# A Hyena and attention encoder layer: the short sequence's second DFT stage computed in quarters of the array, and the filter's real and imaginary parts each stored twice

## The chip, the cores and the metric

The kernel runs on one core of a Trainium2 chip. The metric is device time in microseconds (us) of one execution, lower is better; several runs are taken and the median is compared. The core's engines are named as in the profile: PE (TensorE, matmuls; PEld is its weight load), DVE (VectorE), ACT (ScalarE), POOL (GpSimd) and SP (SyncE, which here only issues DMAs).

## The reference

One encoder layer is applied with the same weights to two sequences: the prompt, 1024 positions (sequence A in the kernel), and the sample, 512 positions (sequence B), both with 1024 channels. After a modulated RMS norm one projection feeds a Hyena branch (768 channels), a dilated attention branch and two gates. The gated branch outputs are merged, projected and added to the input; a squared-ReLU MLP follows. Everything is float32. The change lies in the Hyena branch, a convolution as long as the sequence, whose filter is itself computed by a small network from position features:

```python
def implicit_filter(L, w1, b1, ..., w_out):
    ...
    h_fwd, h_bwd = jnp.split(h, 2, axis=-1)
    h_fwd, h_bwd = h_fwd * decay, h_bwd * decay
    k2 = jnp.concatenate([h_fwd, jnp.zeros((1, D_HYENA), f32), h_bwd[1:][::-1]], axis=0)
    return k2 / jnp.sum(jnp.abs(k2), axis=0, keepdims=True)

def long_conv(u, k2, d):
    L = u.shape[1]
    uf = u.astype(jnp.float32)
    U = jnp.fft.rfft(uf, n=2 * L, axis=1)
    K = jnp.fft.rfft(k2, n=2 * L, axis=0)
    y = jnp.fft.irfft(U * K[None], n=2 * L, axis=1)[:, :L]
    return (y + uf * d.astype(jnp.float32)).astype(u.dtype)

def hyena_branch(z, conv_w, conv_b, ...):
    ...
    x0, x1, v = jnp.split(zc, 3, axis=-1)
    k2 = implicit_filter(L, ...)
    return x0 * long_conv(x1 * v, k2, hyena_d)
```

## The kernel before

**The main stream.** The big projections are a list of units, run in order by `stream` (L483). A unit loads a 128-column piece of a weight (`wdma`, L468), splits it on ACT and DVE into a high and a low fp32r part (`split`, called at L480; ACT's cast is L401, DVE's subtraction L402), and multiplies it in `mm3` (L762), three products for each tile; the matmuls are at L768. Unit i+1's weight is split when unit i begins. The units come in this order: qkv and z of A (`qkvA`, `zhyA`), gates of A (`gateA`), `qkvB`, `zhyB`, `gateB`, then `mixA`, `mixB` (merge and output projection), `ffA`, `ffB`.

**The side work.** Filters (`filtA`, `filtB`), convolutions (`convA`, `convB`), attention, norms and the loading of the Hyena output for the merge (`load_y`, the DMA at L1425) are generators. `pump` advances them between the steps of the units; each `yield` states a cost and a latency on a planned clock, and that clock decides where in the program a piece of side work is written. `LLD` (8.0) is the time that a stage-two step allows for its loads, `LY` (6.0) the time between the product with the filter and the backward DFT. The context holds ACT to the order in which the program is written (`manual_schedule` with the Activation engine). The instructions of the other engines are placed by the framework's scheduler.

**The long convolution.** A transform of 2L points is done in two stages of 32 and Q = L/16 points: Q is 64 for A and 32 for B. Each third of the 768 channels (256 channels) is a step of its own. Stage one goes out to a DRAM tile, stage two reads it back in another order. In stage two a group `eg` holds four 128-row tiles of 256 channels, and each tile is multiplied by its own 128 x 128 matrix (`cmat`, L907, a pool of four buffers). For A (Q = 64) the 128 rows are the real and imaginary part of one residue. For B (Q = 32) they are the real and imaginary parts of two residues l = 0, 1, in the order (part, l, q), and the matrix has zeros wherever the two residues would mix, in half of its entries. A float32 product of 128 x 128 by 256 columns shows as two MATMUL records.

- The filter, `filt_third` (L827): stage one is at L867 in 64 x 64 quarters of the array; stage two (L890 to L902) multiplies at L899, scales on DVE at L900 and stores the spectrum with one DMA of 128 rows per group at L902 into `S.spec[th]`, real rows first, imaginary rows behind.
- The convolution, `conv_gen` (L927): `middle` (L966) loads four pieces of the spectrum (L971, L972), so that `ka` holds the real part in both halves and `kb` the imaginary part in both halves; loads two matrices; multiplies forward at L984, by the spectrum on DVE at L985 to L988, and backward at L995; ACT copies the result (L996, recorded at the helper's line L388) and the stores are at L1001. Each group is handled as two halves `ep` of two tiles with a `yield` between them. Groups of one convolution follow one another (`WMID` is 1). Behind the last group the result is read back at L1008 and multiplied at L1020.
- A has four groups per third, B two. So B has six filter steps, six forward and six backward products, each of four tiles.

These products write to PSUM tiles that `pss2` takes from a pool of four buffers.

## Time and profile before

| what | value |
|---|---|
| median of 3 runs | 2627.82 us (2626.16 to 2630.31) |
| the profiled execution, its own time | 2630.32 us |
| its span, first to last instruction | 2628.5 us |
| mean granted TensorE clock | 0.990 |
| ACT busy | 860.8 us (33%) |
| DMA moved | 351.06 MB, queue q1 busy for 41.1% of 16 engines' span |
| PE work of filter B | from 866.8 to 1086.5 us |
| PE work of convolution B | from 1102.4 to 1362.6 us |

The profile is one execution. A group row gives the line, the engine, the operation, the tiles written and read (`filtB__s` is a PSUM tile that the filter of B made), the shape, the count, then busy time and mean duration, and behind the second bar how long the engine was idle before these instructions and what ended that idle time. A row of the timeline gives the start in us from the span's start, the duration in us, the engine, the line and the count of merged instructions, in brackets the idle time before. A row of the windows gives, for each stretch, its length, the busy time of PE, PEld, DVE, ACT and POOL with counts, the granted clock, the share of the DMA engines and GB/s.

### The profile page before, as it was taken

How to read it: one execution, taken by the hardware profiler on the slowest of the kernel's cores; microseconds unless marked ns; L12 is line 12 of the kernel's file. 1: busy time of each engine (PE TensorE's matmuls, PEld its weight loads, DVE VectorE, ACT ScalarE, POOL GpSimd, SP SyncE). 2: the span in 40 equal slices, each digit the busy share in tenths (PEclk: the TensorE clock that was granted, in tenths of full speed). 3: DMA queues.
4: the chain of work that ended last, by engine and by line, in shares of the span. 5: the costliest groups of instructions: out<-in, count | busy, mean ns of one | idle time of the engine just before them, and what ended most of it. 6: DMA issues, size and time to landing. Idle time of an engine off the chain costs nothing.

```text
span 2628.5 us, 31915 instructions
## 1 busy us (share of the span) xinstructions
PE 2562.4 (97%) x12872; PEld 2061.4 (78%) x12872; DVE 1248.1 (47%) x1626; ACT 860.8 (33%) x1398; POOL 152.0 (6%) x122
## 2 busy tenths in 40 slices
PE   8999999999899999999899989999999999999999
PEld 4677788787788677787788868888888888888887
DVE  4354443744657644653455563333333332554544
ACT  5544323532422444443332442112211221323232
POOL 0111000000010310000022210000000000000000
PEclk9999999999999999999899999999999999999999
DMA  7455575556565344557563531111111112322223
GB/s 269 143 158 182 185 192 169 151 177 175 190 229 188 110 161 141 157 177 233 190 214 114 189 100 61 48 48 49 48 48 48 49 48 80 129 97 96 98 95 104
DMA packets 138106, 351.06 MB, mean 134 GB/s; under 512 B 19016, under 2 KB 50303, under 8 KB 137830
## 3 DMA queue, kind: packets, MB, share of 16 engines
q1 hardware_dynamic: 137670, 348.22, 41.1%
q8 instruction: 102, 1.67, 0.3%
q0 software_dynamic: 288, 0.79, 0.1%
q14 instruction: 46, 0.38, 0.0%
HBM read 280.67 MB, written 71.16 MB: 134 GB/s over the span
## 4 chain that ended last, share of the span: by engine, by line
PE 50%; DVE 1%; DMA 1%; ACT 0%; issue 0%; SPq 0%; DVEq 0%; ACTq 0%
PE ffA__mm L768 27%; PE ffB__mm L768 13%; PE mixA__mm L768 6%; PE mixB__mm L768 2%; PE convB__s L1020 0%; DMA mixA__g<-zhyA__dr 0%; PE gateB__mm L768 0%; DVE mixB__wl L402 0%; ACT mixB__wh L401 0%; PE convB__s L995 0%; DVE mixA__g L402 0%; PE convB__s L984 0%; DMA convB__g<-convB__dr 0%; DVE normA__g L735 0%; DVE mixB__g L1491 0%
## 5 line engine op out<-in xcount | busy, mean ns | idle before, releaser
L768 PE MATMUL ffA__mm<-ffA__g,ffA__wh 128*128 128x512 f32 x1024 | 274.1, 389 | 0.0
L768 PE MATMUL ffA__mm<-normA__g,ffA__wh 128*128 128x512 f32 x992 | 265.1, 389 | 0.0
L768 PEld LDWEIGHTS ffA__mm<-ffA__g,ffA__wh 128*128 128x128 f32 x1024 | 192.0, 188 | 40.4 <-issue 0.4
L768 PEld LDWEIGHTS ffA__mm<-normA__g,ffA__wh 128*128 128x128 f32 x992 | 186.2, 188 | 38.6
L1529 DVE SCALAR_TENSOR_TENSOR mixA__g<-ffA__mm,adam,mixA__g 128x1024 f32<-128x1024 f32 x64 | 82.1, 1283 | 190.1 <-PE ffA__mm L768 190.1
L768 PE MATMUL ffB__mm<-ffB__g,ffB__wh 128*128 128x512 f32 x512 | 157.8, 389 | 0.0
L768 PE MATMUL ffA__mm<-ffA__g,ffA__wl 128*128 128x512 f32 x512 | 157.7, 389 | 0.0
L768 PE MATMUL ffB__mm<-normB__g,ffB__wh 128*128 128x512 f32 x496 | 152.7, 389 | 0.0
L768 PE MATMUL ffA__mm<-normA__g,ffA__wl 128*128 128x512 f32 x496 | 152.7, 389 | 0.0
L401 ACT CAST ffA__wh<-ffA__wr 128x1024 fp32r<-128x1024 f32 x63 | 66.2, 1051 | 256.7 <-PE ffA__mm L768 213.6
L768 PE MATMUL zhyA__mm<-init__g,zhyA__wh 128*128 128x512 f32 x512 | 145.2, 400 | 0.0
L1511 DVE SCALAR_TENSOR_TENSOR ffA__g<-ffA__mm,ffA__g 128x1024 f32<-128x1024 f32 x32 | 39.2, 1224 | 222.8 <-ACT ffA__g L1510 222.8
L768 PE MATMUL gateA__mm<-init__g,gateA__wh 128*128 128x512 f32 x480 | 133.4, 398 | 7.5 <-ACT gateA__wh L401 7.5
L768 PE MATMUL mixA__mm<-mixA__g,mixA__wh 128*128 128x512 f32 x424 | 115.3, 392 | 3.1 <-DVE mixA__g L1463 1.9
L768 PE MATMUL qkvA__mm<-init__g,qkvA__wh 128*128 128x512 f32 x416 | 116.9, 399 | 0.0
L768 PEld LDWEIGHTS zhyA__mm<-init__g,zhyA__wh 128*128 128x128 f32 x512 | 94.2, 188 | 23.6 <-issue 5.7
L768 PEld LDWEIGHTS ffB__mm<-ffB__g,ffB__wh 128*128 128x128 f32 x512 | 96.0, 188 | 20.3 <-ACT ffB__g L401 0.2
L768 PEld LDWEIGHTS gateA__mm<-init__g,gateA__wh 128*128 128x128 f32 x480 | 90.5, 191 | 27.2 <-ACT gateA__wh L401 7.9
L768 PEld LDWEIGHTS ffA__mm<-ffA__g,ffA__wl 128*128 128x128 f32 x512 | 96.1, 188 | 20.0
L1510 ACT ACTIVATE ffA__g<-ffA__mm 128x1024 f32<-128x1024 f32 x32 | 32.9, 1029 | 237.8 <-PE ffA__mm L768 237.8
L768 PEld LDWEIGHTS ffB__mm<-normB__g,ffB__wh 128*128 128x128 f32 x496 | 93.1, 188 | 19.4
L768 PEld LDWEIGHTS ffA__mm<-normA__g,ffA__wl 128*128 128x128 f32 x496 | 93.1, 188 | 19.3
(499 smaller groups left out, 4926.7 us busy)
## 6 DMA issues: line engine op xcount, KB each, us to landing
ada__g<-ada SPq DMA_DIRECT2D x32, 512.0 KB
ffA__wr<-w_up SPq DMA_DIRECT2D x32, 512.0 KB
ffA__wr<-w_dn SPq DMA_DIRECT2D x32, 512.0 KB
ffB__wr<-w_dn SPq DMA_DIRECT2D x32, 512.0 KB
ffB__wr<-w_up SPq DMA_DIRECT2D x30, 512.0 KB
filtA__dr<-filtA__g SPq DMA_DIRECT2D x24, 512.0 KB
convA__g<-filtA__dr SPq DMA_DIRECT2D x48, 256.0 KB
init__g<-ada SPq DMA_DIRECT2D x16, 512.0 KB
```

The source lines that it names most:

```text
L401: A.copy(hi, raw)
L768: T.matmul(ps[:, 512 * c:512 * c + 512], ww[:, sl], xx(k)[:, 512 * c:512 * c + 512], start=k == 0 and p == 0, stop=k == kt - 1 and p == 2)
L1510: A.activation(r, ps[:, :L], AF.Relu)
L1511: V.scalar_tensor_tensor(r, ps[:, :L], 0.0, r, ALU.max, ALU.mult)
L1529: V.scalar_tensor_tensor(S.h(m), ps[:, :L], mod(S, 5, m), S.h(m), ALU.mult, ALU.add)
```

## The change

For B the rows of stage two are put in the order (l, part, q), so that each 128 x 128 matrix is two 64 x 64 blocks. Only these blocks are kept; a group's matrices shrink from 256 KB to 128 KB. A new function, `stage2_products`, replaces the three places that multiplied in stage two. For A it issues what stood there. For B it takes two PSUM buffers at once and issues the eight 64 x 64 products of a group in one go, in the quarter pattern of L867; in tiles 2 and 3 of a group the two residues come out in swapped halves, and the backward matrices are stored with swapped blocks to bring them back.

For both sequences the filter stores its spectrum as two DRAM tiles, the real part twice and the imaginary part twice, so that the convolution loads `ka` and `kb` with one DMA each. In the filter, A's store is two DMAs of 512 KB per group, B's four of 256 KB.

In B's convolution the two DVE operations on 64 partitions (L986, L987) become four on 32 partitions.

```diff
@@ _stage2
     for m in (fw, bw):
-        m = m.reshape(ntile // 4, 4, 128, 128).transpose(0, 2, 1, 3)
+        if nl == 2:
+            m = np.stack([m[:, :, l, :, :, l, :].reshape(ntile, 64, 64) for l in range(2)], axis=1)
+            if out:
+                m[2::4], m[3::4] = m[2::4, ::-1].copy(), m[3::4, ::-1].copy()
+        m = m.reshape(ntile // 4, 4, 128, 128 // nl).transpose(0, 2, 1, 3)
@@ filt_gen
-        S.spec = [dram((128, nt, 256)) for _ in range(3)]
+        S.spec = [[dram((128, nt, 256)) for _ in range(2)] for _ in range(3)]
@@ filt_third, stage2
             so = g((4, 256))
-            for ep in range(2):
-                ps = pss2()
-                for ee in range(2):
-                    e = 2 * ep + ee
-                    T.matmul(ps[:, ee], cm[:, e], sin[:, e], start=True, stop=True)
+            for ep, ps in stage2_products(S, cm, sin):
                 V.tensor_tensor(so[:, 2 * ep:2 * ep + 2], ps, rn.unsqueeze(1).broadcast_to([128, 2, 256]), ALU.mult)
                 yield 0.9, 0.0
-            dma(S.spec[th][:, 4 * eg:4 * eg + 4], so)
+            for l in range(64 // Q):
+                b0 = stage2_row(S, 0, l)
+                for r, dt in enumerate(S.spec[th]):
+                    p0 = stage2_row(S, r, l)
+                    dma(dt[b0:b0 + 2 * Q, 4 * eg:4 * eg + 4].rearrange("(d q) e c -> q d e c", d=2),
+                        so[p0:p0 + Q].unsqueeze(1).broadcast_to([Q, 2, 4, 256]))
@@ cmat
         cm = wp.tile([128, 4, 128], F32, tag="cm", name=nm("cm"), bufs=4)
+        if src.shape[-1] == 64:
+            cm = cm[:, 0:2].rearrange("p a (b c) -> p (a b) c", b=2)
         dma(cm, src[eg])
         return cm
+    def stage2_row(S, r, l):
+        return 64 * r + S.Q * l if S.Q == 64 else 64 * l + S.Q * r
+
+    def stage2_products(S, w, x):
+        if S.Q == 64:
+            for ep in range(2):
+                ps = pss2()
+                for ee in range(2):
+                    T.matmul(ps[:, ee], w[:, 2 * ep + ee], x[:, 2 * ep + ee], start=True, stop=True)
+                yield ep, ps
+            return
+        ps = pss2(), pss2()
+        for ee in range(2):
+            for ep in range(2):
+                for h in range(2):
+                    o, rs = 64 * (h ^ ep), slice(64 * h, 64 * h + 64)
+                    T.matmul(ps[ep][o:o + 64, ee], w[rs, 2 * ep + ee], x[rs, 2 * ep + ee], start=True, stop=True)
+        yield from enumerate(ps)
@@ stage2_load, and the stores of middle
-                p0 = 64 * r + Q * l
+                p0 = stage2_row(S, r, l)
@@ conv_gen, middle
-            for hf in range(2):
-                dma(ka[64 * hf:64 * hf + 64], S.spec[th][0:64, es])
-                dma(kb[64 * hf:64 * hf + 64], S.spec[th][64:128, es])
+            for t, dt in zip((ka, kb), S.spec[th]):
+                dma(t, dt[:, es])
             if eg == 0:
-                V.tensor_copy(ka[64:65, 0], kb[0:1, 0])
+                V.tensor_copy(ka[Q:Q + 1, 0], kb[0:1, 0])
                 V.memset(kb[0:1, 0], 0.0)
-                V.memset(kb[64:65, 0], 0.0)
+                V.memset(kb[Q:Q + 1, 0], 0.0)
             cm, cb_ = cmat(S.fw, eg), cmat(S.bw, eg)
             yield 0.0, LLD
             y, vv = g((4, 256)), g((4, 256))
-            for ep in range(2):
+            for ep, ps in stage2_products(S, cm, sin):
                 e2 = slice(2 * ep, 2 * ep + 2)
-                ps = pss2()
-                for ee in range(2):
-                    T.matmul(ps[:, ee], cm[:, 2 * ep + ee], sin[:, 2 * ep + ee], start=True, stop=True)
                 V.tensor_tensor(y[:, e2], ps, ka[:, e2], ALU.mult)
-                V.scalar_tensor_tensor(vv[0:64, e2], ps[64:128], -1.0, kb[0:64, e2], ALU.mult, ALU.mult)
-                V.tensor_tensor(vv[64:128, e2], ps[0:64], kb[64:128, e2], ALU.mult)
+                for l in range(nl):
+                    re, im = (slice(stage2_row(S, r, l), stage2_row(S, r, l) + Q) for r in range(2))
+                    V.scalar_tensor_tensor(vv[re, e2], ps[im], -1.0, kb[re, e2], ALU.mult, ALU.mult)
+                    V.tensor_tensor(vv[im, e2], ps[re], kb[im, e2], ALU.mult)
                 V.tensor_tensor(y[:, e2], y[:, e2], vv[:, e2], ALU.add)
                 yield 0.9, LY if ep else 0.0
             del sin, ka, kb, vv
             so = g((4, 256))
-            for ep in range(2):
-                ps = pss2()
-                for ee in range(2):
-                    T.matmul(ps[:, ee], cb_[:, 2 * ep + ee], y[:, 2 * ep + ee], start=True, stop=True)
+            for ep, ps in stage2_products(S, cb_, y):
                 copy(so[:, 2 * ep:2 * ep + 2], ps)
                 yield 0.9, 0.0
```

More of the change, by code (lines that the diff above doesn't have):

```diff
@@ L827, in filt_third @@
     def filt_third(S, th, sall, fwo):
-        J, nt = S.J, S.nt
+        J, Q, nt = S.J, S.Q, S.nt
         cs = slice(256 * th, 256 * th + 256)
@@ L999, in middle @@
                 for l in range(nl):
-                    p0 = 64 * r + Q * l
+                    p0 = stage2_row(S, r, l)
                     dma(v2[r, l][:, 4 * eg:4 * eg + 4], so[p0:p0 + Q])
```

## The prediction

> **What bounds the kernel now.** I read the page's busy times first, then the windows by stage, then single groups and the timeline at the places that the change touches.
>
> ```profile
> span 2628.5 us, 31915 instructions
> PE 2562.4 (97%) x12872; PEld 2061.4 (78%) x12872; DVE 1248.1 (47%) x1626; ACT 860.8 (33%) x1398; POOL 152.0 (6%) x122
> ```
>
> PE is the bound over the whole; DVE and ACT have room on the average. An average isn't enough, so here are the stretches: filter A, filter B, convolution B up to 1235 us, and a short one behind it. The columns are length, PE, PEld, DVE, ACT and POOL busy, clock, DMA share and GB/s.
>
> ```profile
> 120.00:310.00 190.00, 185.48 (x1315) 142.85 (x1315) 92.02 (x129) 73.75 (x164) 25.48 (x26) 1.00 0.56 178
> 900.00:1090.00 190.00, 187.73 (x1198) 142.97 (x1197) 103.20 (x165) 92.57 (x200) 23.84 (x23) 1.00 0.43 136
> 1090.00:1235.00 145.00, 143.03 (x737) 116.31 (x736) 69.45 (x109) 57.54 (x116) 0.00 (x0) 1.00 0.61 190
> 1235.00:1281.00 46.00, 32.49 (x132) 26.79 (x131) 17.16 (x19) 13.72 (x18) 0.00 (x0) 0.78 0.70 232
> ```
>
> In filter B and in most of convolution B, PE is busy for 187.73 of 190 and 143.03 of 145 us: what PE is spared there moves everything behind it forward. The exception is 1235 to 1281, with 13.5 us idle and a clock of 0.78. There a chain of other engines is late, and a microsecond of PE work is not a microsecond of time.
>
> **Products of sequence B.** How many records there are, and how long a group takes before:
>
> ```profile
> L899 PE MATMUL filtB__s<-filtB__g,filtB__cm x48: 377/379/381, 937.4 to 1086.5; 128*128 128x256 f32 x48
> L984 PE MATMUL convB__s<-convB__g,convB__cm x48: 377/379/455, 1149.7 to 1334.4; 128*128 128x256 f32 x48
> L995 PE MATMUL convB__s<-convB__g,convB__cm x48: 377/378/483, 1160.1 to 1344.8; 128*128 128x256 f32 x48
> ...
> 1254.87 0.39 PE L768 MATMUL gateB__mm<-normB__g,gateB__wl 128*128 128x512 f32 x1
> 1255.10 1.02 PE L995 MATMUL convB__s<-convB__g,convB__cm 128*128 128x256 f32 x4
> 1255.77 0.81 PE L768 MATMUL gateB__mm<-normB__g,gateB__wh 128*128 128x512 f32 x2
> 1256.42 1.03 PE L995 MATMUL convB__s<-convB__g,convB__cm 128*128 128x256 f32 x4
> 1257.10 0.58 PE L768 MATMUL gateB__mm<-normB__g,gateB__wl 128*128 128x512 f32 x1
> 1257.52 0.63 PE L768 MATMUL gateB__mm<-normB__g,gateB__wh 128*128 128x512 f32 x2
> ```
>
> 3 x 48 records at eight per group are 18 groups. The shown durations overlap in the pipeline, so I price by starts. From 1254.87 to 1257.52 are 2.65 us; they hold one whole group (two runs of four) and four main matmuls. The new shape, 64 x 64 quarters by 256 columns in the same order, is already run by the filter's stage one, also between main matmuls:
>
> ```profile
> 923.62 0.62 PE L768 MATMUL qkvB__mm<-normB__g,qkvB__wh 128*128 128x512 f32 x2
> 924.18 1.09 PE L867 MATMUL filtB__s<-filtB__g,csq 64*64 64x256 f32 x16
> 925.20 0.50 PE L768 MATMUL qkvB__mm<-normB__g,qkvB__wl 128*128 128x512 f32 x1
> 925.54 0.63 PE L768 MATMUL qkvB__mm<-normB__g,qkvB__wh 128*128 128x512 f32 x2
> 926.01 0.40 PE L768 MATMUL qkvB__mm<-normB__g,qkvB__wl 128*128 128x512 f32 x1
> 926.24 0.62 PE L768 MATMUL qkvB__mm<-normB__g,qkvB__wh 128*128 128x512 f32 x2
> ```
>
> From 923.62 to 925.54 are 1.92 us with three main matmuls and one group of 16 quarter records, as many as a group of eight products has. Undisturbed, a main matmul takes 0.23 us (three from 925.54 to 926.24). So a group costs 2.65 - 0.92 = 1.73 us before and 1.92 - 0.69 = 1.23 us after, and 18 groups save 18 x 0.50 = 9.0 us.
>
> The quarters run four at a time only inside the group: four records start (1.02 - 0.38) / 3 = 0.21 us apart before, so sixteen quarters, four at a time, would need 0.86 us; the other 0.37 us go at the two edges, where the shape changes. The Trainium skill, TensorEngine Tiling (Array Packing), Key Properties, says that a change of tiling mode drains TensorE, and its Tiling Modes count four independent tiles at 64 x 64; by the four tiles alone the saving would be 18 x 0.87 = 15.7 us, an estimate, and the forecast below 2614 in place of 2621. The drain agrees with the row, and the sum goes by the row.
>
> **DVE in convolution B.** The two half-height operations become four, and one on 32 partitions costs what one on 64 costs, since 64 cost what 128 do:
>
> ```profile
> L985 DVE TENSOR_TENSOR convB__g<-convB__s,convB__g 128x512 f32<-128x512 f32 x12 | 8.3, 689 | 2.4 <-DMA convB__g<-filtB__dr 1.8 <-PE convB__s L984 0.4
> L986 DVE SCALAR_TENSOR_TENSOR convB__g<-convB__s,convB__g 64x512 f32<-64x512 f32 x12 | 8.3, 693 | 0.4
> L987 DVE TENSOR_TENSOR convB__g<-convB__s,convB__g 64x512 f32<-64x512 f32 x12 | 8.2, 684 | 0.3
> ...
> 1222.41 0.69 DVE L986 SCALAR_TENSOR_TENSOR convB__g<-convB__s,convB__g 64x512 f32<-64x512 f32 x1
> 1223.13 0.69 DVE L987 TENSOR_TENSOR convB__g<-convB__s,convB__g 64x512 f32<-64x512 f32 x1
> ```
>
> They start 0.72 us apart. Two more in each of 12 halves are 24 x 0.72 = 17.3 us more DVE work, 2.9 us in each of six middle steps. DVE is busy for 69 of 145 us, so this is no throughput. It is latency: the backward group now needs both halves of `y`, so it begins 2.9 us later than the second half did, unless PE was late itself. Behind it wait ACT's copies (written order), the stores on SP, and behind those the next group's loads. Until 1235 PE has gate matmuls to do in the meantime; what ACT's order then allows is this, at the end of the first third:
>
> ```profile
> 1183.78 0.59 ACT L388 COPY convB__g<-convB__s 128x512 f32<-128x512 f32 x1 [2.36 <-PE convB__s L995]
> ...
> 1186.04 1.23 DVE L402 TENSOR_TENSOR gateB__wl<-gateB__g,gateB__wh 128x1024 fp32r<-128x1024 f32 x1 [4.95 <-ACT gateB__wh L401]
> ...
> 1189.73 0.61 PE L768 MATMUL gateB__mm<-normB__g,gateB__wh 128*128 128x512 f32 x2
> ```
>
> The weight behind the copy is ready at 1187.27 and used at 1189.73: 2.5 us of cover against 2.9. I take nothing exposed here, at most 0.5 us a step.
>
> **The stretch from 1235 to 1281.** These rows carry it:
>
> ```profile
> 1234.13 0.59 SPq L971 DMA_DIRECT2D convB__g<-filtB__dr  x1
> 1234.77 0.59 SPq L972 DMA_DIRECT2D convB__g<-filtB__dr  x1
> ...
> 1240.05 1.02 PE L984 MATMUL convB__s<-convB__g,convB__cm 128*128 128x256 f32 x4
> 1241.10 0.33 SPq L909 DMA_DIRECT2D convB__cm<-c_fw_b  x1
> 1241.53 0.38 SPq L1425 DMA_DIRECT2D mixA__g<-zhyA__dr  x1
> 1245.19 1.04 ACT L401 CAST mixA__g<-mixA__g 128x1024 fp32r<-128x1024 f32 x1 [13.25 <-DMA mixA__g<-zhyA__dr]
> 1247.72 1.22 PE L768 MATMUL gateB__mm<-normB__g,gateB__wh 128*128 128x512 f32 x2 [3.88 <-ACT gateB__wh L401]
> ...
> 1249.28 5.98 PE gateB__mm L768 x16
> ...
> 1272.62 7.06 PE L1020 MATMUL convB__s<-csq,convB__g 128*128 128x64 f32 x32 [8.77 <-DMA convB__g<-convB__dr]
> ```
>
> SP's matrix load L909 waits for a buffer that the second half of the forward group frees; behind it in SP's queue stands a load for `mixA`, on which ACT's cast waits, and behind that the next gate weight: PE idles 3.88 us. Then the convolution's own end (copy, store, load back) costs 8.77 us idle. Three effects meet here. Forward products in one go free the buffer some 3 us sooner. Two DVE chains, of this group and the one before, are 2.9 us longer each: up to 5.8 later. Two issues of about 0.6 us fewer stand before the group: 1.2 sooner. So the end of the chain lies between 4 us sooner and 6 us later than PE alone would bring it; since the `mixA` cast also stands ahead of the DVE chain, most of the 3 us reach it, and I take 5.8 - 1.2 - 2.6 = 2 us later.
>
> **Stores and loads.** In filter A twelve more 512 KB stores are issued, in B eighteen more DMAs and 3 MB; the convolutions issue 24 and 12 fewer. PE in filter A loses 4.5 of 190 us in all and DMA stands at 0.56; 6.3 MB on top of 178 GB/s x 190 us = 34 MB make it about 0.66. Loads of weights have cover; I take 0, at best 1 us gained from fewer issues, at worst the 8.8 us of the one wait above that a DMA causes. Filter B's two PSUM buffers at once: 0, PE having main work while it waits.
>
> **Sum.** -9.0 + 2.0 = -7.0 us. The profiled execution took 2630.32 us, so it would take 2623.3; it lies 2.5 us above the median of the runs, so the median goes from 2627.82 to 2621.
>
> **The rivals.** (1) The queue is the larger part. If the forward group in one go takes away the whole of the 3.88 us wait, PE doesn't slow down behind it either: the clock is 0.78 in this stretch, and the 16 gate matmuls from 1249.28 on take 5.98 us, 2.3 more than at 0.23 each. Then -9.0 - 3.9 - 2.3 = -15.2, 2613. For it: L909 follows L984 directly. Against it: the 8.77 us behind would still have to be waited for.
>
> (2) The chain decides the stretch alone. Filter B's six groups, the first third's four and four of the second third run before or in it; if the loads, at 0.70 of the DMA engines, set its end, their 7 us are lost and the last third's four groups remain: -2.0, 2626. For it: 13.5 us idle there. Against it: the loads are issued when PE's progress frees buffers, so they move too.
>
> (3) Slower: the longer DVE chain comes through to PE in all six middle steps, by ACT's written order, each holding the next gate or merge weight: 6 x 2.9 = 17.3, net +8.3, 2636. It decides from 9.0 / 6 = 1.5 us exposed per step on. For it: 2.5 us cover against 2.9. Against it: before 1235 PE lost only 2 us in all, and the scheduler may place other matmuls first. The Trainium skill has a rule on this side, TensorEngine Tiling (Array Packing), PSUM Bottleneck: tiling speeds TensorE up but not the emptying of PSUM; here the DVE work that empties it even grows.
>
> (4) The quarters don't overlap, for instance because input rows lie differently: 16 x 0.21 = 3.4 us per group, +30, 2655. L867 is this very shape, so hardly.
>
> **How the numbers follow.** The forecast has 0.48, its own range 2617 to 2625; (1) 0.18, (2) 0.17, (3) 0.14, (4) 0.03. A measurement of this kernel can tell 0.2% from no change, 5.3 us: faster is below 2622.6. Of the forecast 0.36 lie there and 0.12 above, so faster 0.36 + 0.18 = 0.54, same 0.12 + 0.17 = 0.29, slower 0.17. The range reaches from a little below (1), 2610, to 2632, which takes in (2) and the nearer part of the DMA bound and leaves out most of (3) and (4).
>
> **What would show it.** 96 records each at L899's, L984's and L995's successors for B, of 64*64, in runs of 16 that cost about 1.23 us between main matmuls; 48 DVE operations of 32x512 at about 0.69 us; the wait of L909 for the forward products gone, and the 3.88 us idle shorter; L1020 behind it still waiting for its load. Wrong if PE's idle time between 1150 and 1370 us grows by over 9 us, if the groups cost 1.7 us, or if PE begins to wait for weights in filter A.

## The result and the profile after

| kernel | median | lowest to highest | runs |
|---|---|---|---|
| before | 2627.32 us | 2626.16 to 2630.31 | 4 |
| after | 2640.64 us | 2636.92 to 2642.65 | 4 |

The change makes the kernel slower by 13.3 us: the ratio is 1.005, with a 95% interval from 1.0038 to 1.0063. The forecast was 2621 and its range ended at 2632, so the prediction was wrong, in its sign too. The nearest of its cases was rival (3), 2636.

The profiled execution of after took 2639.55 us. Its page begins:

```profile
span 2637.8 us, 32235 instructions
PE 2567.5 (97%) x13016; PEld 2044.8 (78%) x13016; DVE 1263.1 (48%) x1650; ACT 859.9 (33%) x1398; POOL 152.3 (6%) x122
```

The shares stand as they stood; DVE has 24 instructions and 15 us more. The windows of the four stretches of the prediction, with the same columns:

```profile
120.00:310.00 190.00, 182.80 (x1282) 139.63 (x1283) 89.77 (x126) 72.78 (x163) 25.44 (x26) 0.98 0.63 188
900.00:1090.00 190.00, 186.28 (x1246) 136.70 (x1245) 102.80 (x166) 93.76 (x203) 25.62 (x24) 1.00 0.46 142
1090.00:1235.00 145.00, 141.43 (x761) 108.82 (x760) 75.53 (x119) 54.97 (x113) 0.00 (x0) 1.00 0.59 189
1235.00:1281.00 46.00, 34.36 (x154) 24.74 (x152) 21.70 (x25) 13.25 (x17) 0.00 (x0) 0.88 0.61 203
```

Busy time hides where the time went, since a product that is drawn out or cut up counts as busy. A better ruler is the main stream: both kernels have the same 9504 main matmuls in one order. How much later the n-th of them starts after than before, both traces taken from the span's start:

| at (us, before) | 240 | 330 | 720 | 890 | 1105 | 1150 | 1235 | 1281 | 1330 | 1365 | 2600 |
|---|---|---|---|---|---|---|---|---|---|---|---|
| later by (us) | -1.2 | 10.7 | 2.2 | 2.5 | 1.4 | 2.5 | 7.6 | 4.9 | 10.1 | 9.6 | 9.7 |

Three things are to be seen. Filter A loses 12 us between 240 and 330; 8.5 of them are given back by 720, 3.7 of these where PE waited before anyway, for the first weights of A's gates (7.5 us before, 3.8 after). Filter B, from 890 to 1105, gains 1.1. Convolution B, from 1150 to 1365, loses 7, most of it at the first group of the last third: 4.2 us late at 1315, 10.1 at 1330. (The profiled execution of before lay 3 us above its median and that of after 1 us below, so the ends differ by 9.7 here and by 13.3 in the medians.)

**The products.** The group row of convolution B after:

```profile
L939 PE MATMUL convB__s<-convB__g,convB__cm 64*64 64x256 f32 x192 | 23.4, 400 | 5.4 <-DVE convB__g L1016 5.2
```

PE's idle time ahead of these products is 5.4 us, nearly all ended by DVE's sum into `y`; L984 and L995 together had 1.5 before. The row of filter B has none:

```profile
L939 PE MATMUL filtB__s<-filtB__g,filtB__cm 64*64 64x256 f32 x96 | 7.2, 390 | 0.0
```

A whole group of the filter in PE's timeline of after:

```profile
1026.15 0.39 PE L774 MATMUL zhyB__mm<-normB__g,zhyB__wl 128*128 128x512 f32 x1
1026.47 1.09 PE L939 MATMUL filtB__s<-filtB__g,filtB__cm 64*64 64x256 f32 x16
1027.50 0.73 PE L774 MATMUL zhyB__mm<-normB__g,zhyB__wh 128*128 128x512 f32 x2
1028.07 0.39 PE L774 MATMUL zhyB__mm<-normB__g,zhyB__wl 128*128 128x512 f32 x1
```

From 1026.15 to 1028.07 are 1.92 us with three main matmuls at 0.23: the group costs 1.23 us, as forecast. The ruler agrees: over three groups that stay whole the lateness falls from 1.92 to 1.38 us and on to 0.80 (at 1017, 1025 and 1032) and from 1.51 to 1.00 (1077 to 1083), 0.5 to 0.6 us each. Between 1033 and 1044 other side work, which runs there in another order, takes 0.7 back. A backward group of the convolution looks different:

```profile
1182.83 0.39 PE L774 MATMUL gateB__mm<-normB__g,gateB__wl 128*128 128x512 f32 x1
1183.14 1.08 PE L939 MATMUL convB__s<-convB__g,convB__cm 64*64 64x256 f32 x8
1184.16 0.73 PE L774 MATMUL gateB__mm<-normB__g,gateB__wh 128*128 128x512 f32 x2
1184.73 0.39 PE L774 MATMUL gateB__mm<-normB__g,gateB__wl 128*128 128x512 f32 x1
...
1186.39 1.08 PE L939 MATMUL convB__s<-convB__g,convB__cm 64*64 64x256 f32 x8
```

It is torn in two, main matmuls between the pieces. From 1182.83 to 1184.73 are 1.90 us with three main matmuls, so eight records alone cost 1.2 us, as much as sixteen together. The eight belong to one half, and a half holds only two of the four quarters of the array. All six backward groups are torn so, 2 x 1.2 in place of the 1.73 before; of the six forward groups four are in two pieces.

**DVE.** The four operations on 32 partitions take what the two on 64 took each, as forecast:

```profile
L1014 DVE SCALAR_TENSOR_TENSOR convB__g<-convB__s,convB__g 32x512 f32<-32x512 f32 x24 | 16.5, 689 | 1.0 <-DMA convB__g<-filtB__dr 0.6
L1015 DVE TENSOR_TENSOR convB__g<-convB__s,convB__g 32x512 f32<-32x512 f32 x24 | 16.4, 685 | 0.3
```

The same place of the second third in both timelines, first operation of the chain, its last sum, and the backward product behind it; before:

```profile
1221.69 0.69 DVE L985 TENSOR_TENSOR convB__g<-convB__s,convB__g 128x512 f32<-128x512 f32 x1
...
1227.73 0.68 DVE L988 TENSOR_TENSOR convB__g<-convB__g,convB__g 128x512 f32<-128x512 f32 x1
1228.56 1.10 PE L995 MATMUL convB__s<-convB__g,convB__cm 128*128 128x256 f32 x4 [0.29 <-DVE convB__g L988]
```

And after:

```profile
1227.47 0.69 DVE L1011 TENSOR_TENSOR convB__g<-convB__s,convB__g 128x512 f32<-128x512 f32 x1
...
1232.43 1.08 PE L939 MATMUL convB__s<-convB__g,convB__cm 64*64 64x256 f32 x8 [0.97 <-DVE convB__g L1016]
...
1236.28 0.68 DVE L1016 TENSOR_TENSOR convB__g<-convB__g,convB__g 128x512 f32<-128x512 f32 x1
1237.11 1.08 PE L939 MATMUL convB__s<-convB__g,convB__cm 64*64 64x256 f32 x8 [1.56 <-DVE convB__g L1016]
```

The chain took 6.72 us and takes 9.49, 2.8 us more. PE waits for it at both halves. The place of the largest loss, the first group of the last third, looks like this after:

```profile
1325.19 1.08 PE L939 MATMUL convB__s<-convB__g,convB__cm 64*64 64x256 f32 x8 [1.44 <-DVE convB__g L1016]
...
1327.29 1.22 DVE L1488 TENSOR_TENSOR mixA__g<-mixA__mm,mixA__g 128x1024 f32<-128x1024 f32 x1
...
1328.57 1.65 PE L774 MATMUL mixA__mm<-mixA__g,mixA__wh 128*128 128x512 f32 x3 [2.30 <-DVE mixA__g L1488]
```

PE waits 1.44 us for the sum into `y` and then 2.30 us for an operation of the merge that stands behind the chain in DVE's queue. Before, this merge operation stood behind a shorter chain, and PE waited 0.56 us for it, at 1320.93.

**The stretch from 1235 to 1281.** The cast for `mixA` still stands ahead of the gate weight, and the wait for it is shorter, 3.05 us against 3.88:

```profile
1251.45 1.04 ACT L407 CAST mixA__g<-mixA__g 128x1024 fp32r<-128x1024 f32 x1 [11.21 <-DMA mixA__g<-zhyA__dr]
1253.98 1.22 PE L774 MATMUL gateB__mm<-normB__g,gateB__wh 128*128 128x512 f32 x2 [3.05 <-ACT gateB__wh L407]
```

**Filter A.** The issues of the spectrum's store on SP, with the shortest, median and longest in ns, before:

```profile
L902 SPq DMA_DIRECT2D filtA__dr<-filtA__g x12: 319/326/382, 143.5 to 306.0; - x12
```

And after, where there are twice as many and the median is over three times as long:

```profile
L909 SPq DMA_DIRECT2D filtA__dr<-filtA__g x24: 602/1108/2242, 143.4 to 322.5; - x24
```

These times hold more than the form of the store. Two that meet a quiet queue take 0.6 us each (two in 1.29 us at 248.08); four close together take 2 us each, and the two plain loads right behind them 1.6 us each, where one took 0.48 us before (at 225.58):

```profile
224.54 7.91 SPq L909 DMA_DIRECT2D filtA__dr<-filtA__g  x4
232.50 3.32 SPq L951 DMA_DIRECT2D filtA__g<-filtA__dr  x2
```

From 224 to 240 us the DMA engines are at 0.90 in after and at 0.54 before, which the mean of 0.63 over the filter hides. Two waits in PE's timeline of after, which filter A did not have before, come from loads behind these stores in SP's queue. The second is such a load itself. The first comes by a longer way: the filter's group behind its loads starts at 245.44 (at 232.66 before), and an attention product, ACT's copy of it and the ACT and DVE operations on the main stream's PSUM tile stand behind that group:

```profile
253.73 2.04 PE L774 MATMUL zhyA__mm<-init__g,zhyA__wh 128*128 128x512 f32 x4 [3.49 <-DVE zhyA__g L1069]
319.06 1.97 PE L931 MATMUL filtA__s<-filtA__g,filtA__cm 128*128 128x256 f32 x8 [2.98 <-DMA filtA__g<-filtA__dr]
```

Behind the first wait the main products start 0.43 us apart for a while, in place of 0.23; the granted clock from 254 to 262 us is 0.64.

### The profile page after: what moved, and what is told of

Its sections match the earlier page's. It is cut to its first block, busy times and chain, and to the rows that moved or that the text cites. A ratio compares the mean times of both kernels' runs of the same rounds, so it can differ in the third digit from the quotient of the medians.

```text
span 2637.8 us, 32235 instructions
## 1 busy us (share of the span) xinstructions
PE 2567.5 (97%) x13016; PEld 2044.8 (78%) x13016; DVE 1263.1 (48%) x1650; ACT 859.9 (33%) x1398; POOL 152.3 (6%) x122
## 4 chain that ended last, share of the span: by engine, by line
PE 77%; DVE 4%; ACT 2%; DMA 2%; issue 1%; POOL 0%; SPq 0%; DVEq 0%; ACTq 0%; POOLq 0%
PE ffA__mm L774 26%; PE ffB__mm L774 13%; PE mixA__mm L774 6%; PE gateA__mm L774 6%; PE qkvA__mm L774 4%; PE zhyB__mm L774 3%; PE qkvB__mm L774 3%; PE mixB__mm L774 2%; PE zhyA__mm L774 2%; PE gateB__mm L774 2%; PE convA__s L931 1%; PE convA__s L1045 1%; PE convB__s L939 1%; DMA mixA__g<-zhyA__dr 1%; PE attA__s L1303 0%
```

## The experiments

Three theories were set against each other. **Chain**: the four DVE operations, being ahead of the backward product, cost most. **Torn**: the groups cut in two eat what the quarters spare. **Stores**: the doubled spectrum costs, by SP's time to issue or by its bytes. Each kernel ran in alternation with the kernel before on the same chip; the ratio is to those runs.

| kernel | median | before there | ratio, 95% interval |
|---|---|---|---|
| bw_whole | 2643.28 | 2627.48 | 1.0063 [1.0050, 1.0075] |
| a_old | 2634.40 | 2627.48 | 1.0027 [1.0017, 1.0038] |
| store_only | 2631.94 | 2627.48 | 1.0019 [1.0010, 1.0028] |
| dve_only | 2639.56 | 2627.48 | 1.0042 [1.0030, 1.0055] |
| q_nodve | 2620.65 | 2627.85 | 0.9972 [0.9961, 0.9983] |
| q_nodve_whole | 2618.07 | 2627.85 | 0.9962 [0.9949, 0.9974] |
| store_plain | 2633.41 | 2627.85 | 1.0020 [1.0011, 1.0028] |
| fwd_cols | 2626.64 | 2627.85 | 0.9996 [0.9987, 1.0005] |
| store_twice | 2629.84 | 2626.30 | 1.0010 [1.0001, 1.0019] |
| dve_side | 2627.72 | 2626.30 | 1.0001 [0.9992, 1.0010] |
| a_old_pool | 2631.72 | 2626.30 | 1.0021 [1.0012, 1.0030] |
| pool_only | 2622.17 | 2626.30 | 0.9983 [0.9974, 0.9992] |
| dve_mid | 2633.18 | 2626.23 | 1.0029 [1.0017, 1.0040] |
| filt_cols | 2625.05 | 2626.23 | 0.9997 [0.9988, 1.0006] |
| filt_pool | 2619.94 | 2626.23 | 0.9975 [0.9966, 0.9984] |
| fwd_pool | 2619.21 | 2626.23 | 0.9976 [0.9967, 0.9984] |

**bw_whole: the backward groups kept whole.** To the kernel after:

```diff
-                V.tensor_tensor(y[:, e2], y[:, e2], vv[:, e2], ALU.add)
+                if nl == 1:
+                    V.tensor_tensor(y[:, e2], y[:, e2], vv[:, e2], ALU.add)
+                elif ep:
+                    V.tensor_tensor(y, y, vv, ALU.add)
```

> The changed kernel, but in B the last addition of y is done once for both halves, so that all eight backward products of a group become ready together. Theory T (the groups are torn): after the change each backward group runs as two runs of eight quarter records of one half each, 1.22 us a run, 2.44 us in place of the 1.23 us of a whole group; here the six are whole again, 6 x 1.2 = 7.3 us less, 2633 us. Theory D (the four DVE operations lengthen the chain, and it comes through to PE): the chain is at most 0.9 us of DVE shorter in all, 2640 us, or later, since the first half now waits for the second.

All six groups ran as sixteen records, and the time went to 2643.28, not down. PE's waits from 1090 to 1400 us for the sum into `y`, for the merge and for the low halves of the weights were 5.2, 3.0 and 1.0 us in after; here they are:

```profile
PE convB__s L939 <- DVE convB__g L1019: 2.1, 2, 1.8
PE mixA__mm L774 <- DVE mixA__g L1491: 6.3, 2, 4.2
PE gateB__mm L774 <- DVE gateB__wl L408: 3.6, 3, 2.3
```

PE waits less for `y` and more for what stands behind the chain on DVE. Tearing is not what loses by itself: as long as the chain is this long, the time goes elsewhere when the groups stay whole.

**a_old: sequence A's stores and loads as before**, the rest as changed:

```diff
+            if S is SA:
+                dma(S.spec[th][0][:, 4 * eg:4 * eg + 4], so)
...
+            if S is SA:
+                for hf in range(2):
+                    dma(ka[64 * hf:64 * hf + 64], S.spec[th][0][0:64, es])
+                    dma(kb[64 * hf:64 * hf + 64], S.spec[th][0][64:128, es])
```

> The changed kernel with sequence A's spectrum stored once and loaded in four pieces as before; B as changed. Theories T and D both put the loss in B; the main stream of the changed kernel is 2.4 us late when A's convolutions end, so 2638 us. Theory S (the doubled stores carry the loss): A's stage is up to 11 us late before it catches up, 2630 us.

2634.40, so A's stores and loads carry 6.2 of the 13.3 us. The other 7 remain.

**store_only and dve_only: the kernel before with one part of the change each**, the doubled stores (with the two loads of the change, not shown) and the four DVE operations:

```diff
-            dma(S.spec[th][:, 4 * eg:4 * eg + 4], so)
+            for r, dt in enumerate(S.spec[th]):
+                dma(dt[:, 4 * eg:4 * eg + 4].rearrange("(d q) e c -> q d e c", d=2),
+                    so[64 * r:64 * r + 64].unsqueeze(1).broadcast_to([64, 2, 4, 256]))
```

```diff
-                V.scalar_tensor_tensor(vv[0:64, e2], ps[64:128], -1.0, kb[0:64, e2], ALU.mult, ALU.mult)
-                V.tensor_tensor(vv[64:128, e2], ps[0:64], kb[64:128, e2], ALU.mult)
+                for p in range(0, 64, Q):
+                    V.scalar_tensor_tensor(vv[p:p + Q, e2], ps[64 + p:64 + p + Q], -1.0, kb[p:p + Q, e2], ALU.mult, ALU.mult)
+                    V.tensor_tensor(vv[64 + p:64 + p + Q, e2], ps[p:p + Q], kb[64 + p:64 + p + Q, e2], ALU.mult)
```

> The kernel before with the spectrum stored twice and loaded with one DMA each, for A and B, and nothing else. Theories T and D: the 2.4 us by which A is late, 2630 us. Theory S: most of the 13 us, 2638 us or more.

> The kernel before with B's two half-height DVE operations of a middle step as four on 32 partitions, and nothing else: 24 more DVE operations of about 0.69 us. Theory D: they come through to PE, 10 to 17 us, 2638 to 2644 us. Theory T: they are mostly covered, 0 to 4 us, 2627 to 2631 us.

The stores alone cost 4.5 us; the DVE operations alone, with every product on the whole array, cost 12.1 us, nearly as much as the whole change. PE's waits from 1090 to 1400 us in dve_only (us in total, times, longest):

```profile
PE convB__s L1021 <- DMA convB__g<-convB__dr: 6.3, 3, 5.1
PE mixA__mm L768 <- DVE mixA__g L1464: 5.9, 2, 3.0
...
PE convB__s L996 <- DVE convB__g L989: 2.6, 2, 2.0
PE gateB__mm L768 <- DVE gateB__wl L402: 2.6, 4, 1.0
```

Before, the waits for the merge (L1463 there), for the sum into `y` and for the low halves of the weights were 1.9, 0.3 and 0.9 us. The largest increase, 4.0 us, is in the wait for the merge. That points to DVE's queue, in which weights and merge operations stand behind the chain; dve_side and dve_mid, below, test it in part.

**q_nodve and q_nodve_whole: the changed products without the further DVE operations.** To a_old; the second has the single sum of bw_whole too. Both leave B's cross products of real and imaginary parts out of what they compute, since the wrong parts meet:

```diff
-                for l in range(nl):
-                    re, im = (slice(stage2_row(S, r, l), stage2_row(S, r, l) + Q) for r in range(2))
-                    V.scalar_tensor_tensor(vv[re, e2], ps[im], -1.0, kb[re, e2], ALU.mult, ALU.mult)
-                    V.tensor_tensor(vv[im, e2], ps[re], kb[im, e2], ALU.mult)
+                V.scalar_tensor_tensor(vv[0:64, e2], ps[64:128], -1.0, kb[0:64, e2], ALU.mult, ALU.mult)
+                V.tensor_tensor(vv[64:128, e2], ps[0:64], kb[64:128, e2], ALU.mult)
```

> From the changed kernel with sequence A's stores and loads as they were before (2634.4 us): sequence B's cross products of real and imaginary parts go back to two DVE operations of 64 partitions per half, where the change has four of 32. With the changed order of rows the wrong parts meet, so the cross products of B are left out of what is computed; the number of DVE operations, their shapes and the products on PE are those of the comparison. Theory D (the four operations on DVE cost about 12 us, as in the run that added them to the kernel before) expects 2634.4 - 12 = 2622 us, within 3. The rival T (the quarter groups torn in two by the order of the instructions carry the loss, and the DVE work is mostly covered) expects that little goes: 2631 or later.

> The run before this one (cross products of B on 64 partitions, so left out as there), with one further edit: the last sum into y is made once for both halves, so that the sixteen records of each backward group stay together. If a torn group costs 2 x 1.22 = 2.44 us and a whole one 1.23, up to six groups give back 6 x 1.21 = 7.3 us; one of them is whole already, so at most 6 us: 2616 us by that. If PE's first half only waits for the second, as the run with the single sum and four operations showed, the gain is lost in waits: 2622 to 2626, no better than the run before.

2634.40 becomes 2620.65: the operations cost 13.75 us in the changed kernel (14.1 when each is set against its own runs of the kernel before). The single sum gives another 2.6, to 2618.07, near the 2616 that the torn groups' price gave. In q_nodve three of the six backward groups ran already without main matmuls between their halves, so the 13.75 us hold what these three groups spare as well. The row of the products shows what the waits shrink to, from 5.4 us after to 1.8 in q_nodve:

```profile
L941 PE MATMUL convB__s<-convB__g,convB__cm 64*64 64x256 f32 x192 | 20.4, 391 | 1.8 <-DVE convB__g L1021 1.5 <-DMA convB__g<-convB__dr 0.2
```

**dve_side and dve_mid: the same DVE work at two other places.** Both add 24 operations of 32 x 512 to the kernel before; the first behind the last sum into `y`, the second between the last read of the PSUM buffer and the sum:

```diff
+                if nl == 2 and ep:
+                    for p in range(0, 128, 32):
+                        V.tensor_tensor(vv[p:p + 32, e2], ka[p:p + 32, e2], kb[p:p + 32, e2], ALU.mult)
```

```diff
+                for p in (0, 32) if nl == 2 else ():
+                    V.tensor_tensor(kb[p:p + 32, e2], ka[p:p + 32, e2], ka[p:p + 32, e2], ALU.mult)
                 V.tensor_tensor(y[:, e2], y[:, e2], vv[:, e2], ALU.add)
```

> The kernel before, with four further DVE operations of 32 x 512 per four tiles of sequence B behind the last sum into y (on inputs already in SBUF, into a tile that is read no more): 24 operations and some 16.5 us more of DVE, as in the run with four in place of two, but none of them ahead of a backward product. Theory 'queue' (DVE works in order, and the operations hold up weights and sums of the main stream behind them) expects about the +12 us of that run: 2636 to 2640. Theory 'chain' (the backward products come later, and ACT's copies and stores behind them) expects no more than 2 us: 2627.5 to 2630.

> The kernel before, with two further DVE operations of 32 x 512 per half of sequence B's middle steps, placed between the last read of the PSUM buffer and the sum into y; they read and write SBUF only (rows that are read no more). 24 operations, 16.5 us of DVE, as in the two earlier runs, again ahead of the backward products, but the PSUM buffer of the forward products is not held by them. Theory 'chain' (what counts is that y, the backward products and what is stored and loaded behind them come later) expects about the +12 us of the run with four operations in place of two: 2635 to 2640. Theory 'PSUM' (those operations hold the PSUM buffer, on which other products wait) expects about nothing, as the operations behind the sum gave: 2626 to 2629.

Behind the chain the operations cost nothing that can be measured, 1.0001, though they took 18.5 us of DVE, as its group row shows:

```profile
L991 DVE TENSOR_TENSOR convB__g<-convB__g,convB__g 32x512 f32<-32x512 f32 x24 | 18.5, 771 | 0.4
```

Ahead of the sum they cost 7.0 us. So the amount of DVE work is not the cause, and its place in the chain is. The waits of PE for `y` and for the merge, from 1090 to 1400 us, in dve_mid:

```profile
PE convB__s L997 <- DVE convB__g L990: 4.3, 3, 2.9
PE mixA__mm L768 <- DVE mixA__g L1465: 2.5, 1, 2.5
```

And in dve_side, where the wait for `y` is what it was before:

```profile
PE mixA__mm L768 <- DVE mixA__g L1466: 2.1, 2, 1.3
PE convB__s L998 <- DVE convB__g L988: 0.2, 1, 0.2
```

The queue theory is not refuted by this, because dve_side hardly tests it. At the place of the largest loss the merge operations stand ahead of the added work there:

```profile
1316.94 1.23 DVE L1466 TENSOR_TENSOR mixA__g<-mixA__mm,mixA__g 128x1024 f32<-128x1024 f32 x1
...
1319.81 4.88 DVE L991 TENSOR_TENSOR convB__g<-convB__g,convB__g 32x512 f32<-32x512 f32 x4
```

And behind four of the six groups DVE waits at least 0.75 us for its next operation, so the added work held nothing up. What is shown is that the operations cost when they stand ahead of the last sum, with whatever DVE has queued behind it.

Of dve_only's 12.1 us, dve_mid has 7.0. Of the 5 between them, 3.4 appear in the profile as the wait for the merge (5.9 against 2.5 us). The rest may be the PSUM buffer, which the operations hold longer in dve_only, or the spread of the order of instructions from one kernel to the next; no run separates these, and the two intervals overlap.

**pool_only and a_old_pool: the sums into `y` on POOL**, in the kernel before and in a_old:

```diff
-                V.tensor_tensor(y[:, e2], y[:, e2], vv[:, e2], ALU.add)
+                (G_ if nl == 2 else V).tensor_tensor(y[:, e2], y[:, e2], vv[:, e2], ALU.add)
```

> The changed kernel with sequence A's stores and loads as before (2634.4 us), with sequence B's 12 sums into y on POOL, which is idle in that stage; POOL takes about 1.3 to 1.5 us for 128 x 512 where DVE takes 0.68. Theory 'queue' expects DVE's 8.2 us less in its queue to give back about half of the 12 us: 2628 to 2630. Theory 'chain' expects the chain, longer by 0.7 us and a hand-over per half, to cost: 2636 or more.

> The kernel before, with sequence B's 12 sums into y on POOL. Theory 'queue' expects a gain, up to 8.2 x 12 / 16.5 = 6 us: 2622 to 2626. Theory 'chain' expects 2628 to 2633, the chain being longer by about 0.7 us and a hand-over per half.

pool_only is 4.1 us faster than the kernel before, where the queue theory had expected 2622 to 2626 and the chain theory 2628 to 2633. a_old_pool lies 5.4 us above the kernel before where a_old lies 6.9, a difference that the intervals do not separate. The chain theory had counted on a longer chain, and at the place shown above there is none: it runs from 1218.66 to 1225.32 in pool_only, 6.66 us against 6.72: POOL's sum is slow, yet the first half's sum and a weight no longer stand between DVE's other operations.

```profile
1218.66 0.69 DVE L985 TENSOR_TENSOR convB__g<-convB__s,convB__g 128x512 f32<-128x512 f32 x1
...
1223.02 2.30 POOL L988 TENSOR_TENSOR convB__g<-convB__g,convB__g 128x512 f32<-128x512 f32 x1 [0.79 <-DVE convB__g L987]
```

So the run does not decide between the theories, but PE's waits speak for the queue: that for `y` grows from 0.3 to 3.1 us, that for the merge shrinks from 1.9 to 0.2. Where the 4 us come from is only read from the profile: by the ruler 4.6 of them appear between 1235 and 1281 us, where PE's wait for the last read-back is 3.7 us in place of 8.8.

```profile
PE convB__s L1020 <- DMA convB__g<-convB__dr: 3.7, 1, 3.7
```

**store_plain and store_twice: the same bytes, issued otherwise.** Four plain stores of 64 partitions per group; and the whole tile of 128 partitions stored twice as it was stored once, with the four loads of before:

```diff
+            for r, dt in enumerate(S.spec[th]):
+                for h in range(2):
+                    dma(dt[64 * h:64 * h + 64, 4 * eg:4 * eg + 4], so[64 * r:64 * r + 64])
```

```diff
+            for dt in S.spec[th]:
+                dma(dt[:, 4 * eg:4 * eg + 4], so)
```

> The kernel before, with the filter storing real and imaginary parts twice and the convolutions loading with two DMAs, as in the change, but each store a plain one of 256 KB to one place (four per four tiles) where the change has two of 512 KB that read their source twice. The bytes written are the same. Theory 'issue' (the stores cost because SP takes 1.29 us to issue one that reads its source twice, against 0.33 for a plain one) expects most of the 4.5 us of the run with the doubled store to go: 2627.5 to 2629 us. Theory 'bytes' (the 9.4 MB more written cost) expects the same as that run, 2632, or more for the further issues.

> The kernel before, with the filter storing its whole tile of 512 KB twice, each time as before (128 partitions, one DMA), and each half of the convolutions' loads reading its own copy; four loads per four tiles as before. The bytes written are those of the change; SP's issues for stores in filter A should take 24 x 0.33 = 8 us in place of 29 (doubled store, two issues) and 36 (four plain issues). Theory 'issue' (SP's time at the stores delays the loads queued behind them) expects 2627.5 to 2629. Theory 'bytes' (the 9.4 MB more delay other transfers) expects 2631 to 2633, as both runs with the doubled store gave.

store_plain did not separate the theories: its stores of half the size take SP 0.96 us each, 48 of them in A, so neither bytes nor issue time fell:

```profile
L904 SPq DMA_DIRECT2D filtA__dr<-filtA__g x48: 466/955/1522, 143.2 to 326.0; - x48
```

store_twice did cut the issue time, to 0.42 us for each of 24:

```profile
L903 SPq DMA_DIRECT2D filtA__dr<-filtA__g x24: 319/423/1267, 143.1 to 313.3; - x24
```

With it, filter A loses 2.2 us by the ruler at 330 us, where store_only loses 11.2 for the same bytes. So in filter A it is the form of the stores and not their bytes alone. The form changes two things at once: SP's time, and the share of the DMA engines from 224 to 240 us, 0.67 here against 0.86 in store_only and 0.93 in store_plain; which of them makes the loads late is not separated. At the end of the kernel the difference is smaller: 3.5 us slower than before against store_only's 4.5, and the two intervals overlap. How much of the end is form and how much bytes stays open.

**fwd_cols and filt_cols: quarters without the rest.** Pieces of 64 x 32 let the output rows fall where the kernel before has them, so DVE, stores and the backward products stay as before. fwd_cols has filter and forward products so, filt_cols the filter's alone:

```diff
+        ps = pss2(), pss2()
+        for ee in range(2):
+            for ep in range(2):
+                for i in range(4):
+                    h, r = i % 2 ^ ep, i // 2
+                    rs = slice(64 * h, 64 * h + 64)
+                    T.matmul(ps[ep][32 * i:32 * i + 32, ee], w[rs, 2 * ep + ee, 32 * r:32 * r + 32],
+                             x[rs, 2 * ep + ee], start=True, stop=True)
```

> The kernel before, with only the filter's and the forward products of sequence B in quarters: matrices of 64 x 64 are used in pieces of 64 x 32 whose output rows are put where the kernel before has them, so the backward products, all DVE operations and all stores and loads of the spectrum stay as they were. 32 records per group; the same shape in the filter of A took 1.23 us for 32. If products in quarters pay and only the DVE work and the stores cost, 12 groups give 12 x 0.50 = 6.0 us: 2621.5. If groups are torn in two by the order, each torn one gives back 0.5 or loses 0.7: 2624 to 2628. Theory 'mode' (quarters don't pay between main products) expects 2627.5 or more.

> The kernel before, with only the filter's second stage of sequence B in quarters (64 x 32 pieces, 32 records per group, output rows where they were but for the two halves of the sequence's rows, exchanged in every third and fourth tile); the convolutions' products, DVE operations, stores and loads as before, with matrices that take this order. If a whole group saves 0.50 us between main products, and the filter's groups stay whole, 6 x 0.50 = 3.0 us go: 2624. If quarters don't pay by themselves, no difference: 2627.

Neither differs measurably from before. In filt_cols the main stream gains 2.0 us over filter B by the ruler, 1.1 of them from the two groups between 950 and 1033 us, less from the others; if that is a gain, it is within the measurement's uncertainty. In fwd_cols four of the convolution's six forward groups were torn, and from 1105 to 1365 us the main stream gains only 0.5 us more.

**filt_pool and fwd_pool: what helped, together.** The two kernels above with pool_only's edit.

> The run before with the 12 sums into y of sequence B on POOL as well (4 us less by itself): if the two gains add up, 2627 - 3 - 4 = 2620, and this is the fastest kernel; if the shorter chain uses up what the filter spared, 2622.

> Filter and forward products of sequence B in 64 x 32 pieces (1 us less by itself, within the noise), and the 12 sums into y on POOL. If the convolutions' torn groups cost what the filter's whole ones spare, about 2621 to 2623, no better than the run before; if the earlier chain also sets the PSUM buffers free, so that the groups stay whole, 12 x 0.50 + 4 = 10 less: 2617.

Both beat the kernel before by 6 to 7 us and lie over 20 below the changed kernel's median. The two cannot be told apart, so the forward products in quarters add nothing that can be measured.

## Why the prediction was wrong

**What the runs add up to.** From 2627.85: the quarters with B's doubled stores and whole backward groups, -9.8 (q_nodve_whole); torn backward groups, +2.6; the DVE operations, +13.75; A's stores and loads, +6.2. The sum is +12.8, the distance from the kernel before to the changed one in these runs. It has to be: each step begins where the one before it ends, so the sum proves nothing, and its use is in the sizes. The effects measured on the kernel before, 12.1 for the DVE operations and 4.5 for the stores, with -9.8 and 2.6 from here, would give 9.4 (with B's stores counted twice), so the sizes are good to a few us only.

**Products: the size held, for whole groups.** The term was 18 x 0.50 = 9.0 us, and a whole group costs 1.23 us as read from L867. The prediction took every group as whole. Five of filter B's six are; in the convolution the order of instructions puts main matmuls between the halves of all six backward groups, whose second half's input comes later, and a half alone costs as much as the group. What would be lost if a group were split was never priced, though the prediction itself said that the quarters overlap only inside it.

**DVE: the step that failed.** "I take nothing exposed here, at most 0.5 us a step." The runs show 13.75 / 6 = 2.3 us a step in the changed kernel and 2.0 in the kernel before (dve_only). The 2.5 us of cover was read at one place, behind ACT's copy at the end of the first third, and from one follower, the next weight. At 1228 us the backward product itself starts 0.15 us after the sum (1227.73 + 0.68 = 1228.41, then 1228.56): no cover at all, and the row was there to be read. Rival (3) had the size nearly right, 2.9 us in all six steps, but by way of ACT's written order, and PE's wait for ACT's cast did not grow (3.88 us, then 3.05). What the runs show is that the operations cost when they stand ahead of the sum and not when they stand behind it, and that PE then waits on DVE: for `y` (0.3 us before, 5.2 after) and for the merge behind the chain (1.9 before, 3.0 after, 5.9 in dve_only, 6.3 in bw_whole). How the loss is shared among these and the read-back is not settled.

The Trainium skill, TensorEngine Tiling (Array Packing), PSUM Bottleneck, says that tiling speeds up TensorE and not the emptying of PSUM. The trace agrees: the groups' products became cheaper where they stayed whole, while the DVE chain that takes them from PSUM went from 6.72 to 9.49 us at the place shown.

**"DVE is busy for 69 of 145 us, so this is no throughput."** That was right as an average, and dve_side shows it: 18.5 us more DVE work at no cost. It says nothing of the moments at which a merge operation or a weight stands behind the chain.

**Stores: taken at 0, measured 6.2.** The bound was right, "at worst the 8.8", but the value was chosen by the share of the DMA engines, which did come out about as forecast (0.63 in filter A against 0.66). The mean was the wrong figure: from 224 to 240 us the share is 0.90, a store that reads its source twice takes SP 1.1 us to issue in the median where the plain one takes 0.33, and the filter's own loads, decay and weights stand behind it. The prediction counted the issues and did not price them. Its sign of being wrong, PE beginning to wait in filter A, came true, though not for weights: PE waited for the filter's loads and, through ACT and DVE, for a PSUM tile. (The 1.29 us in the expectation of store_plain is the length of a row of two issues in the timeline of after.)

**The stretch from 1235 to 1281.** Forecast 2.0 later; by the ruler PE is 7.6 us late at 1235 and 4.9 at 1281, so the stretch took up 2.7 us of lateness. L1045 still waits for its load, 5.3 us, and the 3.88 us wait became 3.05, as "what would show it" said. That PE's idle time between 1150 and 1370 us would grow by over 9 us was a poor sign to name: torn groups count as busy, and PE is busy for 202.66 of the 220 us before and for 1.9 us less after:

```profile
1150.00:1370.00 220.00, 202.66 (x917) 166.77 (x916) 91.48 (x109) 66.75 (x89) 15.61 (x6) 0.95 0.67 213
1150.00:1370.00 220.00, 200.74 (x976) 151.26 (x975) 104.66 (x133) 62.96 (x85) 12.93 (x5) 0.95 0.61 203
```

**Rival (4).** Its 30 us more would give 2658, not 2655; nothing rests on it, as the quarters did overlap (1.23 us a group).

## What to carry to other kernels

An operation added between a product and the next product that needs it is latency, whatever the engine's share of busy time: look at how long the follower waits at every such place, not at one, and at what else the engine has queued behind the chain. Packing the array pays only for instructions that stay together; price the pieces as well, since half of a packed group can cost as much as the whole. And a DMA costs its queue the time to issue it: read that duration for the form that the change uses, not for the one that it replaces, and where such DMAs follow closely on one another.

## What the runs showed of the hardware

- On DVE these float32 operations over 512 columns took 0.69 us on 32, 64 or 128 partitions.
- Issuing a 512 KB store from 128 partitions took SP 0.33 us in the median, one of 256 KB from 64 partitions 0.96 us (store_plain), and one of 512 KB that reads 64 partitions twice 1.1 us, 0.6 where the queue was quiet and about 2 in a run of four.
- Sixteen records of 64 x 64, or thirty-two of 64 x 32, cost 1.23 us between main products; eight of the 64 x 64 that use only two quarters cost 1.2 us as well.
- POOL's sum of 128 x 512 took 1.27 to 2.30 us where DVE's took 0.68, and the kernel before was still 4.1 us faster with it (pool_only).
